# A hybrid retention and sparse-attention layer: five edits to the order of the mixer's side work

## The chip, the cores and the metric

The kernel runs on one core of a Trainium2 chip. The metric is the device time of one execution in microseconds (us); of the kernel before, the median of three runs is 1142.47 us (1141.43 to 1143.33). The engines are TensorE (PE, with weight loads as PEld), VectorE (DVE), ScalarE (ACT), GpSimd (POOL) and SyncE (SP), which issues most of the transfers. Each runs its instructions in program order and waits on semaphores for the others. Matrix products land in PSUM, eight banks of 512 fp32 columns for each partition.

## The reference, cut to what matters

One encoder layer for a prompt (512 tokens) and a sample (32 tokens), with shared weights: a feed-forward half step, a mixer, a second feed-forward half step, each followed by a LayerNorm of the residual stream. A vector c, multiplied by the matrix w_cond, gives shift, scale and gate of each step (nine pieces of 1024 columns). The mixer projects its input once and feeds two groups of heads:

```python
h = modulate(x, sh2, sc2)
z = jnp.einsum('btd,de->bte', h, w_in)      # retention q,k,v,gate | attention q,k,v | indexer q,k,weights
# retention, 4 heads: scores = (q k^T) * D ; S_new = gamma^C * S + k^T (decay * v) ; inner + q S * decay
# attention, 8 heads: rotary on 16 of 64 dims; an indexer score picks the 128 best keys of each query
s = jnp.einsum('bqhd,bsd->bqhs', iq, ik) * (IDX_DH ** -0.5)
index_score = jnp.einsum('bqh,bqhs->bqs', iw, jax.nn.relu(s))
_, idx = lax.top_k(index_score, topk)       # then softmax attention over the chosen keys
x = post_norm(x, jnp.einsum('btm,md->btd', mixed, w_out), 1.0 + gt2, 1.0, ln2_g, ln2_b)
```

The sample attends to 512 cached keys and its own 32. All is fp32.

## The kernel before, in words

Activations lie transposed, features on partitions and all 544 tokens (512 + 32) along the free dimension, in two halves of 272 columns. A weight block of 128 x 1024 is loaded in fp32 (`wr`), and split into a rounded part and a rest (`wh`): a cast on ScalarE (L131) and a subtraction on VectorE, GpSimd or in a transfer (L141, L139). Each product takes three matmuls, so a half of a block is a stretch of 8 x 3 = 24 matmuls; `in` is such a stretch of the mixer's projection. All matmuls go through `mm` (L77), transpositions through `turned` (L80), and both keep the order in which they are written. `load` keeps the order of SyncE's loads.

The work beside the projections is written as generators. `project` (L893) computes one 128-column block of the projection in two stretches and calls `tick()` after each, and every generator says with `yield n` after how many ticks it is resumed. So the number of yields sets behind which stretch a generator's matmuls stand in PE's order, and flags (`wait_for`) hold a generator until another has got to a point. Instructions of the other engines are ordered by a scheduler, from their dependencies and priorities; `behind` adds an order where one is wanted.

Around the change:

- **LayerNorm to the mixer's input** (`ln_half`, `ln_to_h`, L300-367). VectorE adds up S and Q over the features (L264, L265), PE sums them over partitions (`pm`, `pv`), a chain of small VectorE steps (L332-L341) makes the reciprocal root, then each of the eight feature blocks h_0 to h_7 gets L364 (VectorE), L366 (ScalarE) and L367 (VectorE). It is done for token half 0, then half 1; the projection of half 0 starts on h_0 and h_1 while half 1's sums run.
- **cond_ahead(7)** (L595) computes piece 7 of c times w_cond ahead of time, as eight multiply-adds over rows of w_cond, each with two VectorE instructions on 128 x 1024 (L605 for the first, L607 for the others). Below, "pieces" 0 to 7 are these eight. 0 to 3 stand ahead of the indexer's rotary turn (`rope_turn`, L926), where VectorE waits for the gathered rows; 4 to 7 stand at 502, 526, 548 and 574 us.
- **The top-k** (`topk`, L1099): 16 rounds (17 for the sample, work['s']) of MAX8 and MATCH_REPLACE8 for each query block; it yields after every second round, and after every round for 's'. The masks are then used by attention.
- **retention(hh)**, one after another for four heads. Its side generator multiplies the sample's k and q into `pz` (`rz` in the profile), VectorE multiplies that with the decay (L1200), PE transposes the sample's k into the same bank (L1201), ScalarE scales the transposition (L1202).
- **pair_inputs(c)**, four pairs of heads: projections, rotary turn, then stacks `aks`, `aqs`; it sets the flag ("stack", c), from which `attention` may start pair c. **attention** takes a pair in three steps n = 0, 1, 2 (logits of 128 and 256 columns, of 384, of 512) and a pipeline of logits (`lg`, bank tag l, two banks), transposition (`pt`, tag t, two) and values (`po`, tag o, one). VectorE reads the logits with the mask in L1278.
- **sample_attention(g)**, for pairs 2g and 2g+1: logits `sl` of the sample, softmax `Psu`, transposition `spt`, values `spo` (tag l).

Of the kernel before, what the change touches and what calls it, by code (L numbers as in the profile page):

```python
# [16 lines left out]
P = 128  # L17
# [22 lines left out]
def encoder_layer_kernel(ctx, tc, xT, cT, wc1, w_e, w_cond, b_condT, lnp, w_gu1, w_dn1, w_in, w_out, w_gu2, w_dn2,  # L40
# [525 lines left out]
    def cond(parts, gaps):  # L566
# [13 lines left out]
        for n, (m, d) in enumerate(todo):  # L580
# [11 lines left out]
                spawn(cond_done(m, accs[m]))  # L592
            yield gaps[n % len(gaps)]

    def cond_ahead(m):  # L595
        acc = [up.tile([P, 1024], F32, name=f"ca{m}_{r}", tag="u") for r in range(2)]

        def part(d):
            return w_cond[d * P:(d + 1) * P, 1024 * m:1024 * m + 1024]

        def add(d, w):
            for r in range(2):
                c = cz[:, d, r:r + 1]
                if d == 0:
                    n = nc.vector.tensor_scalar(acc[r], w, c, None, op0=ALU.mult)  # L605
                else:
                    n = nc.vector.scalar_tensor_tensor(acc[r], w, c, acc[r], op0=ALU.mult, op1=ALU.add)  # L607
                tc.add_manual_dep(n.ins, last["pe"], NOSYNC, reason="pace")

        ws = [up.tile([P, 1024], F32, name=f"wc{m}_{d}", tag="u") for d in range(4)]  # L610
        for d in range(4):
            nc.gpsimd.dma_start(ws[d], part(d))
        yield 6
        for d in range(4):
            add(d, ws[d])
            if d % 2:
                yield 1
        yield 16
        for d in range(4, ND):
            ws.append(up.tile([P, 1024], F32, name=f"wc{m}_{d}", tag="u"))  # L620
            load(ws[d], part(d))
        for d in range(4, ND):
            add(d, ws[d])
            yield 5 if d < ND - 1 else 20
        spawn(cond_done(m, acc))

    def later(n, job):
# [295 lines left out]

    def rope_turn(rp, *zs):
        r = rp[0:32 * len(zs)]
        behind(behind(nc.vector.stream_shuffle(r[:, 1, :], r[:, 0, :], SWAP), "evac"), "norm")  # L926
        nc.vector.tensor_mul(r, r, tabA[0:32 * len(zs)])
        nc.vector.tensor_add(r[:, 0, :], r[:, 0, :], r[:, 1, :])
        for slot, z in enumerate(zs):
            nc.sync.dma_start(z[ROT], rp[32 * slot:32 * slot + 32, 0, :])  # L930
# [35 lines left out]


    hls = [next_w(0) for c in range(4)]
    ensure(1)
    misc = unit("misc")  # L970
    cs = misc[:, 0, 0:12]
    load(cs, csm)
# [5 lines left out]
    tabA, tabR = unit("tabA"), unit("tabR")  # L978
    load(tabA, ropes[0])
    load(tabR, ropes[1])  # L980
    ix, ix2 = unit("ix"), unit("ix2")
    ikd = ix[:, 0, :]
    z = ikd
# [119 lines left out]
    def topk():  # L1103
        for t, rate in ((1, 2), (2, 2), (3, 2), ('s', 1)):
            while ("score", t) not in flags:
                yield 1
            w = work[t]
            for n in range(17 if t == 's' else 16):
                m8 = sm.tile([P, 8], F32, name="m8", tag="m8")
                behind(behind(nc.vector.max(m8, w), "pe"), "norm")  # L1110
                nc.vector.match_replace(w, in_to_replace=m8, in_values=w, imm_value=MARK)  # L1111
                if n % rate == rate - 1:
                    yield 1
            nc.vector.tensor_scalar(w, w, -3.3e38, NEG, op0=ALU.is_gt, op1=ALU.mult)
            if t != 's':
                L = P * (t + 1)
                nc.vector.memset(w[0:64, L - 64:L], NEG)
            flags.add(("mask", t))
# [41 lines left out]
    def retention(hh):  # L1160
        qk = unit("rqk")
        q, k = qk[:, 0, :], qk[:, 1, :]
        project_full(q)
        Dm = unit("Dm")
        Dh = Dm[:, 0, 0:P]
        load(Dh, dec[hh])
        S0 = Dm[:, 1, 0:128]
        load(S0, s0[hh])
        so, so2 = Dm[:, 1, 128:256], Dm[:, 1, 256:384]
        ss = Dm[:, 0, P:P + 32]  # L1170
        project_full(k)
        sa, sb = unit("rsA"), unit("rsB")
        sT, kt = sa[:, 0, 0:512], sa[:, 1, 0:512]
        on = sb[:, 1, 0:512]
        on2 = sb[:, 0, 256:384]
        ks = sb[:, 0, 384:512]
        vu = unit("rv")
        V = vu[:, 0, 0:512]
        vsm = vu[0:32, 1, 0:P]
        St = vu[:, 1, P:4 * P]  # L1180
        rt = ret[hh // 2][:, hh % 2, :]

        def tk(x, t):
            return x[:, t * P:(t + 1) * P]

        def side():
            yield 1 if hh else 2
            ps = bank("l", "rs")
            for t in range(4):
                mm(tk(ps, t), tk(k, t), tk(q, t), start=True, stop=True)  # L1190
            nc.vector.tensor_tensor(sT.rearrange("p (t n) -> p t n", t=4), ps.rearrange("p (t n) -> p t n", t=4),
                                    Dh.unsqueeze(1).to_broadcast([P, 4, P]), op=ALU.mult)
            pk = bank("t", "rkt")
            for t in range(4):
                turned(tk(pk, t), tk(k, t), ident)
            nc.scalar.activation(kt, pk, AF.Copy, scale=gk[:, hh:hh + 1])
            yield 1
            pz = bank("l", "rz")
            mm(pz[0:32, 0:32], k[:, TP:T], q[:, TP:T], start=True, stop=True)
            nc.vector.tensor_mul(ss[0:32], pz[0:32, 0:32], Dh[0:32, 0:32])  # L1200
            turned(pz[0:32, P:2 * P], k[:, TP:T], ident)  # L1201
            nc.scalar.activation(ks[0:32], pz[0:32, P:2 * P], AF.Copy, scale=gks[0:32, hh:hh + 1])  # L1202
            yield from wait_for(("V", hh))
            pu = bank("l", "ru")
            for t in range(4):
                mm(tk(pu, t), tk(kt, t), tk(V, t), start=True, stop=True)
            nc.vector.tensor_copy(tk(St, 0), tk(pu, 0))
            for t in range(1, 4):
                nc.vector.scalar_tensor_tensor(tk(St, t) if t < 3 else so, tk(St, t - 1), GAM[hh] ** P, tk(pu, t),
                                               op0=ALU.mult, op1=ALU.add)  # L1210
            nc.sync.dma_start(st_p[hh], so)
            yield 1
            po = bank("a", "ro")
            for t in range(4):
                mm(tk(po, t), tk(sT, t), tk(V, t), start=True, stop=(t == 0))
                if t:
                    mm(tk(po, t), tk(q, t), tk(St, t - 1), start=False, stop=True)
            po2 = bank("l", "ro2")
            mm(po2[0:32, 0:P], ss[0:32], vsm, start=True, stop=False)
            mm(po2[0:32, 0:P], q[:, TP:T], S0, start=False, stop=True)  # L1220
            ps2 = po2[:, P:2 * P]
            mm(ps2, ks[0:32], vsm, start=True, stop=True)
            nc.scalar.activation(on, po, AF.Copy, scale=gn[:, hh:hh + 1])
            nc.scalar.activation(on2[0:32], po2[0:32, 0:P], AF.Copy, scale=gn[0:32, hh:hh + 1])
            nc.vector.scalar_tensor_tensor(so2, S0, GAM[hh] ** 32, ps2, op0=ALU.mult, op1=ALU.add)
            nc.sync.dma_start(st_s[hh], so2)
            normed = [(on[:, n * P:(n + 1) * P], P) for n in range(4)] + [(on2[0:32], 32)]
            with tc.high_priority():
                w = head_norm(normed)
            yield 2  # L1230
            for j, (x, rows) in enumerate(normed):
                nc.scalar.activation(x, x, AF.Identity, bias=w[:rows, 2, j:j + 1], scale=w[:rows, 1, j:j + 1])
            yield 1
            pt = bank("t", "rot")
            for nt in range(4):
                turned(pt[:, nt * P:(nt + 1) * P], on[:, nt * P:(nt + 1) * P], ident)
            nc.scalar.activation(rt[:, 0:TP], pt, AF.Copy, scale=0.5)
            pt2 = bank("a", "rot2")
            turned(pt2[:, 0:32], on2[0:32], ident[0:32, 0:32])
            nc.scalar.activation(rt[:, TP:T], pt2[:, 0:32], AF.Copy, scale=0.5)  # L1240
            flags.add(("ret", hh))

        spawn(side())
        value_chunk(V, vsm, None, ("V", hh))

# [37 lines left out]
    def pair_inputs(c):  # L1283
# [10 lines left out]
        def roped():  # L1294
# [6 lines left out]
            parts(st[0], q)  # L1301
            for s in range(2):
                nc.gpsimd.tensor_copy(qz[own(s), 32 * s:32 * s + 32], q[own(s), TP:T])
            yield 3 if c == 0 else 1
            flags.add(("stack", c))

        Vs[c] = V
# [13 lines left out]
    def sample_attention(g):  # L1321
# [4 lines left out]
        load(cvt, cv[g])  # L1326
        if g == 0:
            yield 3
        yield from wait_for(("mask", 's'), ("att", 2 * g + 1))
        ps, p2 = bank("a", "sl"), bank("t", "sl2")  # L1330
        for j in range(4):
            c = 2 * g + j // 2
# [21 lines left out]
            nc.scalar.copy(PT2[0:32], pt2[0:32, 0:P])  # L1354
            nc.scalar.copy(PT, pt)
        yield 1
        po = bank("l", "spo")
        pcs = [po[own(j % 2), 32 * (j // 2):32 * (j // 2) + 32] for j in range(4)]
        for e in range(2):
            for t in range(4):  # L1360
# [10 lines left out]
    def attention():  # L1371
# [46 lines left out]
        while tiles or any(pipe):  # L1418
# [6 lines left out]
                values(*pipe[2])  # L1425
            if item:
                logits(*item)
            if pipe[1]:
                turn(*pipe[1])
            pipe = [item] + pipe[:2]  # L1430
# [241 lines left out]
```

## Time and profile before

| | us |
|---|---|
| median of three runs | 1142.47 |
| profiled execution | 1138.22 |
| its span, first to last instruction | 1136.4 |
| PE busy in the span | 1110.4 |
| VectorE busy | 850.0 |
| ScalarE busy | 637.1 |
| GpSimd busy | 196.7 |
| PE's waits for VectorE at `lg` / at `rz` | 5.1 / 4.1 |

The times of all rows are from one profiled execution; us count from its first instruction. "Busy" is the sum of the times in which an engine executed something. A row of a timeline gives start, length, engine, line, operation, tiles, shape and count, and in brackets how long the engine had been idle before and what it waited for. The mixer's projections run from about 404 to 690 us. The mean granted clock of TensorE is 0.993 of full speed.

### The profile page before, as it was taken

How to read it: one execution, taken by the hardware profiler on the slowest of the kernel's cores; microseconds unless marked ns; L12 is line 12 of the kernel's file. 1: busy time of each engine (PE TensorE's matmuls, PEld its weight loads, DVE VectorE, ACT ScalarE, POOL GpSimd, SP SyncE). 2: the span in 40 equal slices, each digit the busy share in tenths (PEclk: the TensorE clock that was granted, in tenths of full speed). 3: DMA queues.
4: the chain of work that ended last, by engine and by line, in shares of the span. 5: the costliest groups of instructions: out<-in, count | busy, mean ns of one | idle time of the engine just before them, and what ended most of it. 6: DMA issues, size and time to landing. Idle time of an engine off the chain costs nothing.

```text
span 1136.4 us, 22804 instructions
## 1 busy us (share of the span) xinstructions
PE 1110.4 (98%) x9059; PEld 1079.3 (95%) x9059; DVE 850.0 (75%) x1766; ACT 637.1 (56%) x1116; POOL 196.7 (17%) x217
## 2 busy tenths in 40 slices
PE   8999999999999999999989999999999999999995
PEld 7999999999999999889878989999999999999995
DVE  5578898788779796788898786799799876910416
ACT  3645656754334464766455768646666666753523
POOL 0111111121100313423110101100111111151110
PEclk9999999999999999999989999999999999999998
DMA  9798878997977455756954687861888677478842
GB/s 358 269 274 218 223 193 227 256 262 249 322 211 170 113 202 146 170 168 151 251 115 125 140 262 192 216 200 29 219 235 225 161 180 186 136 215 180 174 83 80
DMA packets 71164, 221.18 MB, mean 195 GB/s; under 512 B 8624, under 2 KB 12848, under 8 KB 71056
## 3 DMA queue, kind: packets, MB, share of 16 engines
q1 hardware_dynamic: 49456, 151.02, 38.0%
q0 software_dynamic: 21456, 68.56, 33.5%
q8 instruction: 71, 1.16, 0.4%
q14 instruction: 37, 0.30, 0.1%
q10 hardware_dynamic: 144, 0.14, 0.0%
HBM read 208.09 MB, written 9.58 MB: 192 GB/s over the span
## 4 chain that ended last, share of the span: by engine, by line
PE 87%; DVE 6%; DMA 4%; ACT 1%; issue 1%; SPq 0%; DVEq 0%; ACTq 0%
PE dn L77 27%; PE pA L77 16%; PE in L77 14%; PE gu L77 11%; PE pB L77 8%; PE pC L77 4%; DMA we_raw<-in_w_e 3%; PE gu_e L77 2%; DVE wk L1111 1%; DVE m L1110 1%; PE po L77 1%; PE lg L77 1%; PE isc L77 1%; PE pt L80 1%; PE ro L77 0%
## 5 line engine op out<-in xcount | busy, mean ns | idle before, releaser
L77 PE MATMUL dn<-hid,wh_w 128*128 128x272 f32 x2112 | 266.6, 288 | 0.0
L77 PEld LDWEIGHTS dn<-hid,wh_w 128*128 128x128 f32 x2112 | 265.2, 188 | 0.2
L77 PE MATMUL in<-h,wh_w 128*128 128x272 f32 x1392 | 188.3, 292 | 0.0
L77 PEld LDWEIGHTS in<-h,wh_w 128*128 128x128 f32 x1392 | 178.0, 190 | 5.2 <-issue 2.8
L131 ACT CAST wh_w<-wr_w 128x1024 fp32r<-128x1024 f32 (+1 forms) x102 | 102.9, 1013 | 100.1 <-PE dn L77 84.2
L77 PE MATMUL gu<-h,wh_w 128*128 128x272 f32 x960 | 121.1, 288 | 0.0
L77 PEld LDWEIGHTS gu<-h,wh_w 128*128 128x128 f32 x960 | 120.6, 188 | 0.0
L589 DVE SCALAR_TENSOR_TENSOR ca<-wc,cz,ca 128x1024 f32<-128x1024 f32 x84 | 107.4, 1298 | 0.0
L77 PE MATMUL pA<-hs,wh_s 128*128 128x272 f32 x720 | 100.3, 288 | 0.0
L77 PEld LDWEIGHTS pA<-hs,wh_s 128*128 128x128 f32 x720 | 93.8, 188 | 0.0
L138 ACT ACTIVATE wh_w<-wh_w 128x1024 fp32r<-128x1024 f32 (+1 forms) x80 | 81.5, 1023 | 1.6
L286 DVE SCALAR_TENSOR_TENSOR xs<-dn,C,xs 128x272 f32<-128x272 f32 (+2 forms) x24 | 9.0, 404 | 81.6 <-PE dn L77 81.6
L680 POOL DMA_DIRECT2D wh_g<-in_w_gu x30 | 26.1, 871 | 240.8 <-ACT wh_g L679 164.1
L714 ACT COPY s<-pA 128x272 f32<-128x272 f32 x90 | 34.5, 383 | 53.9 <-PE pA L77 53.2
L139 POOL DMA_DIRECT2D wh_w<-in_w_dn x32 | 28.2, 881 | 175.6 <-ACT wh_w L138 134.9
L703 DVE TENSOR_TENSOR wh_s<-wr_g,wh_s 128x1024 fp32r<-128x1024 f32 x30 | 36.7, 1224 | 19.4 <-ACT wh_s L702 19.4
L77 PE MATMUL pA<-h,wh_g 128*128 128x272 f32 x360 | 50.1, 288 | 0.0
L77 PE MATMUL pB<-hs,wh_u 128*128 128x272 f32 x360 | 49.8, 287 | 0.0
L77 PE MATMUL pC<-h,wh_g 128*128 128x272 f32 x360 | 49.8, 287 | 0.0
L77 PE MATMUL pB<-hs,wh_s 128*128 128x272 f32 x360 | 49.8, 287 | 0.0
L77 PE MATMUL pA<-h,wh_s 128*128 128x272 f32 x360 | 49.7, 287 | 0.0
L702 ACT CAST wh_s<-wr_g 128x1024 fp32r<-128x1024 f32 x30 | 31.5, 1050 | 30.0 <-DVE wr_g L698 30.0
(331 smaller groups left out, 2052.9 us busy)
## 6 DMA issues: line engine op xcount, KB each, us to landing
wc<-in_w_cond SPq DMA_DIRECT2D x52, 512.0 KB, 6.6
wr_w<-in_w_in SPq DMA_DIRECT2D x33, 512.0 KB, 4.6
wr_g<-in_w_gu SPq DMA_DIRECT2D x30, 512.0 KB, 3.6
wr_u<-in_w_gu SPq DMA_DIRECT2D x30, 512.0 KB, 4.4
wh_g<-in_w_gu POOLq DMA_DIRECT2D x30, 512.0 KB, 6.5
wr_w<-in_w_dn SPq DMA_DIRECT2D x32, 448.0 KB, 4.4
wh_w<-in_w_in POOLq DMA_DIRECT2D x27, 512.0 KB, 7.2
wr_w<-in_w_gu SPq DMA_DIRECT2D x24, 512.0 KB, 7.4
```

Source lines behind the costliest of these rows:

```text
L77: ordered("pe", nc.tensor.matmul(*a, **kw))
L80: ordered("pe", nc.tensor.transpose(*a))
L131: c = nc.scalar.copy(hi[:, :n, :], raw[:, :n, :])
L138: nc.scalar.mul(lo[:, :n, :], hi[:, :n, :].bitcast(F32), -1.0)
L139: nc.gpsimd.dma_start(lo[:, :n, :], src, accum_op=ALU.add)
L589: got = nc.vector.scalar_tensor_tensor(acc, ws[n], c, acc, op0=ALU.mult, op1=ALU.add)
L680: nc.gpsimd.dma_start(lo, src, accum_op=ALU.add)
L702: pin(nc.scalar.copy(W[f][:, 0], raw[f]))
L703: pin(nc.vector.tensor_tensor(W[f][:, 1], raw[f], W[f][:, 0].bitcast(F32), op=ALU.subtract))
L714: pin(nc.scalar.copy(s, ps))
L1110: behind(behind(nc.vector.max(m8, w), "pe"), "norm")
L1111: nc.vector.match_replace(w, in_to_replace=m8, in_values=w, imm_value=MARK)
```

## The change

It leaves the number of matmuls and what is computed as they are. Five edits:

1. `ensure(2)` instead of `ensure(1)`: a second w_in block is loaded and split ahead of the mixer's constants.
2. `cond_ahead`: pieces 4 and 5 follow pieces 0 to 3 at once, their two loads stand behind the rotary tables' loads on SyncE's queue (`ahead_more`), and the indexer's rotary turn is ordered behind piece 5. Pieces 6 and 7 come some 40 ticks later.
3. `topk` yields less often for the sample: 12 times in 17 rounds.
4. retention: the transposition of the sample's key is issued ahead of VectorE's reading of `pz`.
5. `pair_inputs` yields 4 instead of 3 for pair 0; `sample_attention` also waits for the flag ("lg", 2), set when the last logits of pair 2 are issued, and its values use the bank tag o instead of l.

```diff
 def cond_ahead(m):
...
+                if d < 6:
+                    last["piece"] = n.ins.name
...
-        yield 6
+
+        def more():
+            d = len(ws)
+            ws.append(up.tile([P, 1024], F32, name=f"wc{m}_{d}", tag="u"))
+            load(ws[d], part(d))
+
+        ahead_more.extend([more] * 2)
+        yield 5
         for d in range(4):
             add(d, ws[d])
             if d % 2:
                 yield 1
-        yield 16
-        for d in range(4, ND):
-            ws.append(up.tile([P, 1024], F32, name=f"wc{m}_{d}", tag="u"))
-            load(ws[d], part(d))
-        for d in range(4, ND):
+        for d in (4, 5):
             add(d, ws[d])
-            yield 5 if d < ND - 1 else 20
+        yield 40
+        more()
+        more()
+        for d in (6, 7):
+            yield 6 if d == 6 else 3
+            add(d, ws[d])
+        yield 3
         spawn(cond_done(m, acc))
...
-        behind(behind(nc.vector.stream_shuffle(r[:, 1, :], r[:, 0, :], SWAP), "evac"), "norm")
+        behind(behind(behind(nc.vector.stream_shuffle(r[:, 1, :], r[:, 0, :], SWAP), "evac"), "norm"), "piece")
...
-    ensure(1)
+    ensure(2)
...
     load(tabR, ropes[1])
+    for more in ahead_more:
+        more()
...
-                if n % rate == rate - 1:
+                if n % rate == rate - 1 if t != 's' else n % 4:
                     yield 1
...
             mm(pz[0:32, 0:32], k[:, TP:T], q[:, TP:T], start=True, stop=True)
+            turned(pz[0:32, P:2 * P], k[:, TP:T], ident)
             nc.vector.tensor_mul(ss[0:32], pz[0:32, 0:32], Dh[0:32, 0:32])
-            turned(pz[0:32, P:2 * P], k[:, TP:T], ident)
...
-            yield 3 if c == 0 else 1
+            yield 4 if c == 0 else 1
...
-        yield from wait_for(("mask", 's'), ("att", 2 * g + 1))
+        yield from wait_for(("mask", 's'), ("att", 2 * g + 1), ("lg", 2))
...
-        po = bank("l", "spo")
+        po = bank("o", "spo")
...
             if item:
                 logits(*item)
+                if item[1] == 2:
+                    flags.add(("lg", item[0]))
```

What that moves is shown at three places. The first is VectorE in the LayerNorm that makes the mixer's input, half 0: a part of its chain, between S and Q of the seventh feature block and the first `ht`. Before:

```order
L264 TENSOR_TENSOR S<-S,xa_3230 128x272
L337 TENSOR_TENSOR lnz<-pv,lny 128x272
L265 TENSOR_TENSOR Q<-Q,sq 128x272
L338 SCALAR_TENSOR_TENSOR pv<-lnz 128x272
L339 SCALAR_TENSOR_TENSOR pv<-pv,lnz 128x272
L341 SCALAR_TENSOR_TENSOR lny<-pv,lny 128x272
```

and now:

```order
L264 TENSOR_TENSOR S<-S,xa_3230 128x272
L337 TENSOR_TENSOR lnz<-pv,lny 128x272
L265 TENSOR_TENSOR Q<-Q,sq 128x272
L338 SCALAR_TENSOR_TENSOR pv<-lnz 128x272
L141 TENSOR_TENSOR wh_w<-wr_w,wh_w 128x1024
L339 SCALAR_TENSOR_TENSOR pv<-pv,lnz 128x272
L341 SCALAR_TENSOR_TENSOR lny<-pv,lny 128x272
```

A weight split (L141) has come in behind L338. Some fifteen rows further, on the same engine, come S and Q of the eighth feature block (h_5 to h_7 are feature blocks of the mixer's input). Before:

```order
L367 SCALAR_TENSOR_TENSOR h_5_4816<-ht,B_3755,h_5_4816 128x272
L364 SCALAR_TENSOR_TENSOR ht<-xa_3230,G_3754,lny 128x272 x2
L264 TENSOR_TENSOR S<-S,xa_3230 128x272
L265 TENSOR_TENSOR Q<-Q,sq 128x272
L367 SCALAR_TENSOR_TENSOR h_6_4817<-ht,B_3755,h_6_4817 128x272
L367 SCALAR_TENSOR_TENSOR h_7_4818<-ht,B_3755,h_7_4818 128x272
```

and now:

```order
L364 SCALAR_TENSOR_TENSOR ht<-xa_3230,G_3754,lny 128x272 x2
L367 SCALAR_TENSOR_TENSOR h_5_4816<-ht,B_3755,h_5_4816 128x272
L367 SCALAR_TENSOR_TENSOR h_6_4817<-ht,B_3755,h_6_4817 128x272
L367 SCALAR_TENSOR_TENSOR h_7_4818<-ht,B_3755,h_7_4818 128x272
L264 TENSOR_TENSOR S<-S,xa_3230 128x272
L265 TENSOR_TENSOR Q<-Q,sq 128x272
```

S and Q stand behind h_6 and h_7 instead of ahead of them.

The second place is VectorE at the first reads of attention's logits (pair 0; `wk_5266` is the prompt's last top-k block). Before:

```order
L1111 MATCH_REPLACE wk_5266<-m_7046,wk_5266 128x512
L1110 MAX m_7104<-wk_5266 128x8
L1278 ISA Pu,mx<-lg,wk_5266 128x128
L1278 ISA mx 128x1
L1111 MATCH_REPLACE wk_5266<-m_7104,wk_5266 128x512
L1270 TENSOR_SCALAR nm<-mx 128x1
```

and now, where `wk_5279` is that block and `wk_5278` the sample's:

```order
L1126 MATCH_REPLACE wk_5279<-m_7140,wk_5279 128x512
L1126 MATCH_REPLACE wk_5278<-m_7182,wk_5278 128x544
L1129 TENSOR_SCALAR wk_5279<-wk_5279 128x512
L1125 MAX m_7185<-wk_5278 128x8
L1132 MEMSET wk_5279 64x64
L1126 MATCH_REPLACE wk_5278<-m_7185,wk_5278 128x544
L1293 ISA Pu,mx<-lg,wk_5279 128x128
L1293 ISA mx 128x1
```

The reads stood amid the block's rounds; now they stand behind its last round, its mask and two of the sample's rounds. Piece 7 of the modulation, which stood some dozen rows ahead of the first read, is gone from there.

The third is PE around the sample's values (`spo`, g = 0). Before, they stood between the values and transpositions of pair 3:

```order
L77 MATMUL spo<-Psu,cvt 64x32 x8
L77 MATMUL spo<-PsT_8604,aV 64x32 x2
L77 MATMUL spo<-Psu,cvt 64x32 x8
L77 MATMUL spo<-PsT_8604,aV 64x32 x2
L77 MATMUL po<-Pu,aV 64x128 x6
L80 MATMUL pt<-cm,Pu 128x128 x8
```

and now ahead of pair 3's first logits:

```order
L80 MATMUL vt<-cm,vz 128x128 x4
L80 MATMUL vts<-cm,vz 32x128
L77 MATMUL spo<-Psu,cvt 64x32 x8
L77 MATMUL spo<-PsT_8322,aV 64x32 x2
L77 MATMUL spo<-Psu,cvt 64x32 x8
L77 MATMUL spo<-PsT_8322,aV 64x32 x2
L77 MATMUL lg<-aks,aqs 128x128 x6
```

The sample's part for pairs 0 and 1 is done one pair earlier than before.

More of the change, by code (lines that the diff above doesn't have):

```diff
@@ L593, in cond @@
             yield gaps[n % len(gaps)]
+    ahead_more = []
     def cond_ahead(m):
```

## The prediction

> **What bounds the kernel now.** I read the engine totals first, then TensorE's waits, then its timeline around each of them, and last VectorE's timeline ahead of them. The engine totals of the page:
>
> ```profile
> PE 1110.4 (98%) x9059; PEld 1079.3 (95%) x9059; DVE 850.0 (75%) x1766; ACT 637.1 (56%) x1116; POOL 196.7 (17%) x217
> ```
>
> TensorE (PE) is busy for 1110.4 of the span's 1136.4 us. The change leaves every matmul in place, so only the 26.0 us in which PE stands idle, and what a lowered clock costs, can move. The waits of PE, grouped by the operation that waits and the one that ends the wait (total, times, longest):
>
> ```profile
> PE lg L77 <- DVE mx L1278: 5.1, 3, 2.5
> PE rz L80 <- DVE Dm L1200: 4.1, 4, 2.8
> PE vts L80 <- ACT Pu L1398: 0.4, 1, 0.4
> ```
>
> These are the three in the mixer: attention's logits (`lg`) waiting until VectorE has read a PSUM bank, the key transposition of retention (`rz`) waiting for VectorE's reading of the score, and one small wait. Together 9.6 us; the rest of the idle time lies at the start and the end, where the change does nothing. PE's timeline shows each (start, length, instruction, then in brackets the idle time before it):
>
> ```profile
> 465.72 0.28 PE L80 MATMUL rz<-cm,rqk 128*32 128x128 f32 x1 [0.70 <-DVE Dm L1200]
> 491.92 0.28 PE L80 MATMUL rz<-cm,rqk 128*32 128x128 f32 x1 [0.34 <-DVE Dm L1200]
> 523.37 0.28 PE L80 MATMUL rz<-cm,rqk 128*32 128x128 f32 x1 [0.27 <-DVE Dm L1200]
> 550.82 0.28 PE L80 MATMUL rz<-cm,rqk 128*32 128x128 f32 x1 [2.79 <-DVE Dm L1200]
> ...
> 581.54 3.25 PE L77 MATMUL in<-h,wh_w 128*128 128x272 f32 x24
> 587.27 0.68 PE L77 MATMUL lg<-aks,aqs 64*128 64x384 f32 x1 [2.47 <-DVE mx L1278]
> 589.12 1.32 PE L77 MATMUL lg<-aks,aqs 64*128 64x384 f32 x5 [1.17 <-DVE mx L1278]
> 590.37 4.88 PE L77 MATMUL in<-h,wh_w 128*128 128x272 f32 x24
> ...
> 642.41 0.79 PE L77 MATMUL lg<-aks,aqs 64*128 64x384 f32 x6
> ...
> 675.78 1.50 PE L77 MATMUL lg<-aks,aqs 64*128 64x512 f32 x6 [1.42 <-DVE mx L1278]
> ```
>
> The pair of waits at 587 costs more than its 2.47 + 1.17 = 3.64 us: the 24 matmuls behind it take 4.88 us instead of the 3.25 of those ahead of it (+1.6), and the five `lg` 1.32 where six take 0.79 undisturbed (+0.5). That is 2.1 us of lowered clock. The windows of 5 us around both long waits (the figure behind POOL's is the granted clock):
>
> ```profile
> 545.00:550.00 5.00, 3.03 (x25) 2.71 (x24) 4.86 (x11) 2.01 (x5) 0.86 (x1) 1.00 1.05 291
> 550.00:555.00 5.00, 4.18 (x35) 4.17 (x35) 4.86 (x13) 1.22 (x3) 0.00 (x0) 1.00 1.05 309
> 585.00:590.00 5.00, 1.56 (x6) 1.10 (x6) 5.00 (x22) 3.48 (x8) 0.87 (x1) 0.72 0.35 72
> 590.00:595.00 5.00, 5.00 (x27) 4.63 (x24) 4.64 (x17) 0.49 (x2) 0.00 (x0) 0.60 0.61 105
> ```
>
> The idle 2.79 us before 550.82 left the clock at 1.00, while the 3.64 us broken by one matmul took it to 0.72 and 0.60.
>
> **The retention swap.** PE's order is the same; what changes is that the transposition no longer follows VectorE's reading of the score in the same bank, but goes ahead of it. All four waits go: 0.70 + 0.34 + 0.27 + 2.79 = 4.1 us. In exchange VectorE's reading (now L1216) waits for one 0.28 us transposition, which ends long before VectorE arrives (head 3: VectorE came 2.79 us after PE). ScalarE's scaled copy of the key (now L1217) has to wait for VectorE instead; behind it on ScalarE are the copies of the value chunk, for matmuls that follow 3.24 us of other work, and it starts no later than before, since before it waited for the same VectorE instruction and a transposition besides. Price: -4.1 us, nothing next in line.
>
> **One more w_in block before the gap.** With `ensure(2)` a block's split, one ScalarE cast and one VectorE subtraction (L141), stands in the middle of the LayerNorm that makes the mixer's input, half 0. VectorE's rows there:
>
> ```profile
> 398.71 0.44 DVE L338 SCALAR_TENSOR_TENSOR pv<-lnz 128x272 f32<-128x272 f32 x1
> ...
> 406.54 0.43 DVE L264 TENSOR_TENSOR S<-S,xa 128x272 f32<-128x272 f32 x1
> 407.24 0.91 DVE L367 SCALAR_TENSOR_TENSOR h<-ht,B,h 128x272 fp32r<-128x272 f32 x2
> ...
> 421.93 1.22 DVE L141 TENSOR_TENSOR wh_w<-wr_w,wh_w 128x1024 fp32r<-128x1024 f32 x1
> ```
>
> and PE's, at the sum over the features (`pm`) that reads S:
>
> ```profile
> 407.03 0.72 PE L77 MATMUL pm<-S,cm 128*128 128x272 f32 x2
> ```
>
> Before, S was ready at 406.54 + 0.43 = 406.97 and PE read it at 407.03: no reserve. Now an L141 (1.22) stands behind L338, and the two L367 that stood behind S (0.91) stand ahead of it. S comes 1.22 + 0.91 = 2.13 later, less about 0.3 for starts that overlap the end of the one before: PE waits 1.85 us that it didn't wait before. Ends: 0.8 us if only the L367 are felt, since the L141 falls into a pause; 2.2 if nothing overlaps. I take 1.85, near the upper end, since VectorE's rows are back to back. The block's load is no part of it: it stands ahead of the mixer's constants on SyncE's queue. The other half's LayerNorm starts later by as much, loses the L141 at 421.93, and PE reaches it later by as much: nothing.
>
> **Two pieces of modulation in the gap.** VectorE stands idle before the rotary shuffle, and six instructions of the same kind give the price of one:
>
> ```profile
> 424.93 7.25 DVE L607 SCALAR_TENSOR_TENSOR ca<-wc,cz,ca 128x1024 f32<-128x1024 f32 x6
> 439.19 0.01 DVE L926 LOAD_MASK_SELECT rp<-rp  x1 [6.43 <-DMA rp<-iqf]
> ```
>
> Four more take 4 x 7.25 / 6 = 4.83 us, in 6.43 us of idle time that the L141 moved away widens: free, as long as the gathered rows don't arrive over 1.6 us earlier; if they do, the rest falls on the indexer's rope, with no PE wait near it in the list above. Their two loads stand on SyncE's queue behind the rotary tables, and one w_in load fewer stands just ahead of the gathers. The pieces leave their old places, and that is what pays at head 3 and in the first attention. Pieces 6 and 7 go into attention's pairs 2 and 3, where VectorE still has pauses; the second of these rows shows one, 1.85 us:
>
> ```profile
> 573.55 1.27 DVE L607 SCALAR_TENSOR_TENSOR ca<-wc,cz,ca 128x1024 f32<-128x1024 f32 x1
> 639.32 0.29 DVE L1278 CUSTOM_DVE_ANT_0 Pu<-lg,wk 128x128 f32<-128x128 f32 x1 [1.85 <-PE lg L77]
> ```
>
> **The first attention.** Logits now start one 24-matmul stretch later, so PE, which was through with the stretch ahead of the second group (`lg` on 384 columns) at 581.54 + 3.25 = 584.8, comes there at 584.8 + 3.2 = 588.0 in the old times. It needs both PSUM banks of the first group read. VectorE's order is new: the reads no longer stand amid the top-k rounds but behind all of them, with two rounds of the sample's top-k pulled in by the faster yield. These rows price that (the first round stands behind the rope, the last row is the last read of the first group before):
>
> ```profile
> 568.52 0.69 DVE L1110 MAX8 m<-wk 128x8 f32<-128x512 f32 x1
> ...
> 581.28 0.69 DVE L1110 MAX8 m<-wk 128x8 f32<-128x512 f32 x1
> 582.80 0.69 DVE L1110 MAX8 m<-wk 128x8 f32<-128x512 f32 x1
> ...
> 588.64 0.42 DVE L1278 CUSTOM_DVE_ANT_0 Pu<-lg,wk 128x256 f32<-128x256 f32 x1
> ```
>
> Nothing changes up to 573.55, where piece 7 stood. From there 8 rounds of the prompt and 2 of the sample at 582.80 - 581.28 = 1.52 us make 15.2, less an estimated 0.7 where another instruction fills the pause inside a round; the two rope results 1.2; the mask's end 0.45: the first read comes at 589.7. Three reads later, of 0.42 us at most, the first bank is free: 590.7. PE waits 590.7 - 588.0 = 2.7, with the second bank 3.0 us, where it waited 3.64. Ends: 2.0 if more rounds overlap, 4.2 if the rotated keys land 1.2 us late. Without a drop of the clock the 2.1 us go too.
>
> The clock is the open part. [...] So I let it keep the clock, by the row nearest in length, at little better than even odds.
>
> **Pairs 1 to 3 and the sample.** The wait of 1.42 us at 675.78 goes: the sample's two reads stood between the two `lg` reads of pair 3 and now stand in pair 2. The 0.41 us on ScalarE in pair 1 becomes about 0.5, between 0 and 1.7 (the 1.85 us pause is the reserve that a later start uses up). In pair 2 the sample's output bank is now shared with attention's own, so PE waits until VectorE has read that; I count about 1.8 us of reserve there (rival 3).
>
> **Sum**, against the profiled execution of 1138.22 us (span 1136.4, 1.8 around it): -4.1 (retention) - 0.64 - 2.1 (first attention and its clock) - 1.42 (pair 3) + 0.1 (pair 1) + 1.85 (LayerNorm) = -6.3 us, so 1131.9. The median of the runs is 4.25 above that execution, 1142.47; the same difference gives **1136.2 us**. A measurement of this kernel can tell 0.2%, 2.3 us, from nothing.
>
> **Rivals.** *1, the clock still falls in the first attention (0.30).* For it: 3.64 us in all did it before, and 3.0 is near. Then the 2.1 us stay: -4.2, 1138.3. [...]
>
> *2, the first attention doesn't wait (0.10).* If the rounds overlap as the interleaved ones do and the keys land early, VectorE is 3 us sooner: -9.3, 1133.2. Against it: ten rounds in a row depend each on the one before.
>
> *3, slower: the shared output bank (0.06).* In pair 2 the sample's values wait for VectorE's reading of attention's output, which stands behind piece 7, the sample's softmax and the rope of pair 3, and that one waits for a DMA. VectorE is in order, so a late DMA holds it all, and then the logits behind PE's wait. The row before:
>
> ```profile
> 653.65 0.70 DVE L928 TENSOR_TENSOR rp<-rp 64x544 f32<-64x544 f32 x1
> 658.44 0.67 DVE L949 TENSOR_TENSOR aks<-aqk,aks 128x512 fp32r<-128x512 f32 x1
> ```
>
> gave 658.44 - 654.35 = 4.1 us and no wait. Every us beyond my reserve of 1.8 is PE's, and a wait past 3.6 brings 2.1 of clock. To come out over 2.3 us slower it must eat 6.3 + 2.3 - 2.1 = 6.5 us: the DMA 8.3 us later than now, 12.4 in all. At that, 1144.8.
>
> *4, it moves waits and gains little (0.10).* The new wait in the LayerNorm at 2.2, the first attention at 4.2 with its clock drop, pair 1 at 1.7: -4.1 + 0.6 - 1.42 + 1.3 + 2.2 = -1.4, 1141.1.
>
> **How the numbers follow.** My case has 0.44, the rivals 0.30, 0.10, 0.06 and 0.10. The range runs from rival 2, 1133.2, less 0.7 for the LayerNorm's low end, to just under rival 4: 1132.5 to 1141.0. Faster by over 2.3 us (below 1140.2) are my case and rivals 1 and 2, less 0.03 for their tails: 0.81; rival 4 and these tails are within 0.2%: 0.13; rival 3 is slower: 0.06.
>
> **What would show it.** In the new profile PE's list has no `rz` row; a row `pm` waiting for S of about 1.9 us stands near 407; `lg` waits for VectorE once, about 3 us near 585, with 24 matmuls behind it at 3.25 us (4.88 if rival 1 holds); no `lg` wait in pair 3; no `spo` row. The forecast is wrong if `pm` doesn't wait, if `spo` or `spt` does, or if PE's idle time in the mixer is over 8 us.

## The result, and the profile after

The changed kernel takes 1135.05 us (median of four runs, 1134.79 to 1135.26) where the kernel before took 1142.9 (four runs, 1141.43 to 1143.62). The ratio is 0.9933 with a 95% interval of 0.9916 to 0.995: 7.85 us less, between 5.7 and 9.6. Forecast were 1136.2 and -6.3 us. That the numbers lie near each other is partly chance: two terms of the forecast were wrong, in opposite directions, as the part on the prediction shows.

The profiled execution of the changed kernel took 1134.79 us, its span is 1133.0. The engine totals:

```profile
PE 1110.3 (98%) x9059; PEld 1079.8 (95%) x9059; DVE 850.6 (75%) x1766; ACT 636.8 (56%) x1116; POOL 196.3 (17%) x217
```

No engine does less work; PE is idle 22.7 us instead of 26.0. PE's waits in the mixer, out of the same grouping as before:

```profile
PE lg L77 <- DVE mx L1293: 3.5, 2, 3.2
PE pm L77 <- DVE S L264: 1.5, 1, 1.5
...
PE pt L80 <- ACT Pu L1413: 0.6, 1, 0.6
```

The `rz` row is gone, `pm` is new, and `pt`, which waits for ScalarE's copy of a transposition in pair 2, was not foreseen. PE's timeline at these places:

```profile
408.95 0.73 PE L77 MATMUL pm<-S,cm 128*128 128x272 f32 x2 [1.52 <-DVE S L264]
...
582.16 3.26 PE L77 MATMUL in<-h,wh_w 128*128 128x272 f32 x24
588.64 1.73 PE L77 MATMUL lg<-aks,aqs 64*128 64x384 f32 x6 [3.22 <-DVE mx L1293]
590.30 5.31 PE L77 MATMUL in<-h,wh_w 128*128 128x272 f32 x24
...
639.31 1.19 PE L77 MATMUL lg<-aks,aqs 64*128 64x384 f32 x6 [0.26 <-DVE mx L1293]
651.31 0.55 PE L80 MATMUL pt<-cm,Pu 128*128 128x128 f32 x3 [0.57 <-ACT Pu L1413]
```

The wait at the second logits group is one piece of 3.22 us now, and the clock falls behind it as it did before: the 24 matmuls that follow take 5.31 us, those ahead 3.26. The windows (the granted clock is the figure behind POOL's):

```profile
585.00:590.00 5.00, 1.78 (x10) 1.30 (x8) 5.00 (x24) 2.11 (x8) 0.08 (x1) 0.81 0.60 105
590.00:595.00 5.00, 5.00 (x24) 4.70 (x22) 5.00 (x21) 0.95 (x4) 0.00 (x0) 0.51 0.00 0
```

Between the two profiled executions the time falls by 1138.22 - 1134.79 = 3.4 us. The mixer's waits make -4.0 of it: -4.1 at `rz`, -1.6 at `lg` (5.1 to 3.5), -0.4 at `vts`, +1.5 at `pm`, +0.6 at `pt`. What PE loses behind the waits of the first attention is nearly the same in both. Without the idle time, its six `lg` and the 24 matmuls behind them take 6.75 us before and 6.90 now (counted to the starts of the next rows, 595.19 and 595.54), where they take 3.9 undisturbed: a loss of 2.8 and of 3.0 us. Some 0.4 us of such a loss is put down to the wait and not to the clock, an estimate from one row: behind a wait of 0.76 us six such `lg` take 1.20 us at a clock of 1.00 (the sample's top-k one tick later, below), and 0.79 undisturbed. At the start of the program, where no edit stands, PE's waits at the modulation (`c`) came out 0.9 us longer. That makes -4.0 + 0.2 + 0.9 = -2.9; where the remaining 0.5 us are is not shown. The other 4.4 us of the 7.85 are not between these two profiles: the kernel before has a median 4.7 us above its profiled execution, the changed one 0.26 us above its own.

### The profile page after: what moved, and what is told of

It reads as the page before. It is cut to its first block, busy times and chain, and to the rows that moved or that the text cites. A ratio compares the mean times of both kernels' runs of the same rounds, so it can differ in the third digit from the quotient of the medians.

```text
span 1133.0 us, 22791 instructions
## 1 busy us (share of the span) xinstructions
PE 1110.3 (98%) x9059; PEld 1079.8 (95%) x9059; DVE 850.6 (75%) x1766; ACT 636.8 (56%) x1116; POOL 196.3 (17%) x217
## 4 chain that ended last, share of the span: by engine, by line
PE 86%; DVE 7%; DMA 5%; ACT 1%; issue 1%; SPq 0%; DVEq 0%; ACTq 0%
PE dn L77 26%; PE pA L77 16%; PE in L77 13%; PE gu L77 11%; PE pB L77 8%; PE pC L77 4%; DMA we_raw<-in_w_e 3%; PE gu_e L77 2%; DVE m L1125 1%; DVE wk L1126 1%; DMA aqk<-rp 1%; PE isc L77 1%; PE ro L77 1%; PE lg L77 1%; PE pt L80 1%
```

## The experiments

Each was timed against the kernel before on the same chip; the ratios are to that. The changed kernel wasn't timed again beside them. The kernel before has medians of 1140.2 to 1141.4 us in these sessions, against 1142.9 in the four runs of the result, so one or two us between one of these runs and the changed kernel are not told apart.

**The kernel before, again, twice.** No edit.

> The kernel before, unchanged, a second time. Its first profiled execution took 1138.2 us while its timed runs took 1141.4 to 1143.6. Theory A (the granted clock falls at a second place in most executions, the 2.8 us wait of retention head 3, and didn't in that one): a profiled execution at 1141 to 1143 us shows a window with a clock of about 0.5 to 0.8 behind 550 us and a slow stretch of 24 matmuls (about 4.9 instead of 3.25 us) there. Theory B (the profiled execution differs in something spread over the whole span, such as transfers at the start): no new place with a lowered clock, and the 4 us stand elsewhere. If this execution is at 1138 again, the two stay open.

> The kernel before once more, for a profile of one of its longer executions (both profiled ones took 1138.2 us, the median is near 1141). If the granted clock falls behind the 2.8 us wait of retention head 3 in those: a window near 550 us at about 0.6, the 24 matmuls there at 4.5 to 5 us, and the mixer longer by 2 to 3 us. Rival: the extra time stands behind the waits of attention (587 or 676 us) or ahead of the mixer. If the profiled execution is a short one again, only the list of times and clocks can speak: time should go up by 2.5 to 3.5 us for each 0.002 that the mean clock falls.

The first: 1140.09 us (ten runs, 1138.18 to 1144.03), ratio 0.9992 (0.9974 to 1.0009), profiled at 1138.18, so as before. The second: 1140.47 (1137.28 to 1144.78), ratio 0.9999 (0.998 to 1.0017), profiled at 1139.18 with a mean clock of 0.991. This profile bears on theory A. PE's timeline there:

```profile
550.59 0.28 PE L80 MATMUL rz<-cm,rqk 128*32 128x128 f32 x1 [2.80 <-DVE Dm L1200]
550.63 4.79 PE L77 MATMUL in<-h,wh_w 128*128 128x272 f32 x24
```

and the window, here and in the first repetition:

```profile
550.00:555.00 5.00, 4.41 (x23) 4.41 (x24) 4.86 (x13) 0.36 (x1) 0.00 (x0) 0.66 1.04 309
```

```profile
550.00:555.00 5.00, 4.12 (x34) 4.11 (x35) 4.86 (x13) 1.17 (x3) 0.00 (x0) 1.00 1.04 305
```

The same kernel, the same wait of 2.8 us, and once the clock stays at 1.00, once it falls to 0.66 and 24 matmuls take 4.79 instead of 3.24 us. So theory A holds for this place: retention's last wait costs 2.8 us in some executions and 4.35 in others. It isn't all of the spread. Of the 85 timed executions of the kernel before on these three chips, the 23 with a mean clock of 0.993 or more have a median of 1139.5 us, the 47 with 0.991 or 0.992 one of 1140.5, the 15 below that one of 1143.6. No profile shows one of the last. The median of all 85 is 1140.5, and only 30 of them reach 1141.43, the lowest of the result's four. Against 1140.5 the changed kernel's 1135.05 would be 5.5 us less, not 7.85.

**The retention swap alone, and everything but the swap.** In the first, the kernel before with only this; in the second, the changed kernel with the opposite:

```diff
+            turned(pz[0:32, P:2 * P], k[:, TP:T], ident)
             nc.vector.tensor_mul(ss[0:32], pz[0:32, 0:32], Dh[0:32, 0:32])
-            turned(pz[0:32, P:2 * P], k[:, TP:T], ident)
```

> The kernel before with the retention swap alone. Theory A (the four waits go, and in the timed runs a drop of the clock at head 3 with them): 4.1 us and 2 to 4 of clock, so about 1135 to 1137 us where before takes 1142.5, and a profiled execution without an rz wait. Theory B (only the 4.1 us of waits): 1138 to 1139. Rival (VectorE passes the delay on to the first attention, which waits longer): 1140 to 1142.

> The changed kernel with the retention swap undone. If the swap carries most of the gain: the four rz waits are back, 4.1 us or more, so 1139 us or more. Rival (the wait of head 3 came from modulation piece 6 standing on VectorE just ahead of the score's reading, and that piece is gone from there): only the three small waits of together 1.3 us come back, 1136 to 1137 us, and no rz wait is over 1 us.

The swap alone: 1133.72 us (nine runs, 1133.03 to 1138.13) where before took 1141.38, ratio 0.9941 (0.9923 to 0.9958). No `rz` row; what is left waits for attention's logits:

```profile
583.71 0.44 PE L77 MATMUL lg<-aks,aqs 64*128 64x384 f32 x1 [2.90 <-DVE mx L1278]
585.56 1.20 PE L77 MATMUL lg<-aks,aqs 64*128 64x384 f32 x5 [1.41 <-DVE mx L1278]
586.69 4.37 PE L77 MATMUL in<-h,wh_w 128*128 128x272 f32 x24
```

That is theory A, which has 5.5 to 7.5 us: the four waits of 4.1 us are worth 6.7 us by the ratio. Three of the nine runs took 1137 to 1138 us, at a mean clock of 0.991 where the others have 0.993 or 0.994; what lowers it in these, no profile shows. Everything but the swap: 1137.04 us, ratio 0.9963 (0.9948 to 0.9978), which is 2.0 us more than with it by the times and 3.4 by the ratios. Its profile is of the longest of its eleven executions (1142.43 us), so only the waits at `rz` are read from it. The wait of head 3 is 0.54 us there, not 2.79:

```profile
554.66 0.28 PE L80 MATMUL rz<-cm,rqk 128*32 128x128 f32 x1 [0.54 <-DVE Dm L1215]
```

So the rival holds in this one. In the kernel before, the two instructions of modulation piece 6 stand on VectorE just ahead of the score's reading:

```profile
547.69 1.27 DVE L607 SCALAR_TENSOR_TENSOR ca<-wc,cz,ca 128x1024 f32<-128x1024 f32 x1
...
549.40 1.28 DVE L607 SCALAR_TENSOR_TENSOR ca<-wc,cz,ca 128x1024 f32<-128x1024 f32 x1
550.60 0.17 DVE L1200 TENSOR_TENSOR Dm<-rz,Dm 32x32 f32<-32x32 f32 x1
```

They make 2.55 us, and with the piece elsewhere 2.25 of the 2.79 us are gone. The swap takes away the rest and the three small waits (1.3 us). The two edits overlap, and their gains don't add.

**The changed kernel without the early block.**

```diff
-    ensure(2)
+    ensure(1)
```

> The changed kernel with ensure(1) as before. If the split in the LayerNorm costs what the profile shows at pm (1.5 us) and brings nothing: the pm wait goes and the time falls by 1.5 us to about 1133.5. Rival (the early block is needed to keep the gap before the rotary turn free for pieces 4 and 5): the split comes back ahead of the pieces, the shuffle comes later, and the time stays or rises by up to 2 us.

1138.73 us, ratio 0.9973 (0.9959 to 0.9986): slower than the changed kernel by 3.7 us by the times, and by more than the rival had. The `pm` wait is gone, but PE now waits for the block's split, which VectorE does behind all the pieces in the gap. VectorE's rows, then PE's:

```profile
424.44 12.04 DVE L609 SCALAR_TENSOR_TENSOR ca<-wc,cz,ca 128x1024 f32<-128x1024 f32 x10
...
439.50 1.21 DVE L141 TENSOR_TENSOR wh_w<-wr_w,wh_w 128x1024 fp32r<-128x1024 f32 x1
```

```profile
440.77 5.52 PE L77 MATMUL in<-h,wh_w 128*128 128x272 f32 x31 [4.04 <-DVE wh_w L141]
```

The clock falls behind this wait (0.66 from 440 to 445 us): 31 matmuls of this shape take 4.13 us elsewhere in this profile and 5.52 here. The early block is what makes the gap usable: 1.5 us at `pm` are the price for not paying 4.0 and the fall here.

**The early block, split without VectorE.** In the changed kernel:

```diff
-        queue_w(w_in[c], lo_eng=nc.vector if c in (4, 17) else None)
+        queue_w(w_in[c], lo_eng=nc.vector if c == 4 else None)
```

> The changed kernel, with the lower half of the second w_in block made by ScalarE and an accumulating transfer instead of VectorE's subtraction (L141). If that subtraction in the LayerNorm's chain is what delays S: the wait of 1.5 us at pm falls to under 0.5, and the time by 1 to 1.5 us, to about 1133.8. Rival (the order of S and Q behind h_6 and h_7 does it, and it stays): still about 0.8 us of wait, 1134.5. If the transfer comes late, a wait at the first matmul that uses the block, up to 4 us.

1133.56 us (four runs, 1131.76 to 1135.14), ratio 0.9935 (0.9911 to 0.9959). The wait at the second `pm` is gone, and the time is about what the first theory has, though the interval doesn't part it from the changed kernel. The profile has a wait of 1.49 us at the first `pm` instead, 16 us earlier and ahead of this edit's work. Two other profiles of this study have a wait there too (2.07 without the swap, 1.41 with attention's start as before), and the one with both edits, below, has none at either `pm`. So VectorE's subtraction makes the second wait, and not the order of S and Q, which was the rival. What makes the first, and whether it varies with the execution, isn't shown:

```profile
392.38 0.72 PE L77 MATMUL pm<-S,cm 128*128 128x272 f32 x2 [1.49 <-DVE S L264]
...
408.59 0.73 PE L77 MATMUL pm<-S,cm 128*128 128x272 f32 x2
```

**The sample's top-k one tick later**, alone and with the edit above:

```diff
+            if t == 's':
+                yield 1
             w = work[t]
```

> The changed kernel, with the sample's top-k starting one tick later, so that none of its rounds stands ahead of the first reads of attention's logits. If the 3.2 us wait at the second logits group comes from these two rounds (3.0 us) and the mask's end (0.4): that wait is under 0.5 us, no window there has a lowered clock (the 24 matmuls behind it at 3.25 instead of 5.31 us), together 5 to 6 us: about 1129.5. Rival (VectorE is behind by more than these rounds, or the sample's mask, a tick later, makes PE wait in pair 2): a gain of under 2 us, 1133 to 1136.

> The two edits of the runs above together. If they act on separate waits, their gains add: 1128 to 1129 us, and PE's waits in the mixer are under 1.5 us in all. [...]

Alone: 1137.36 us, ratio 0.9962 (0.9945 to 0.9978). The wait of 3.22 us fell to 0.76 (the first theory had under 0.5) with a clock of 1.00, and two waits of together 1.08 us came up at the logits of 512 columns. Yet the time rose, beyond what either had. The rows show where it went:

```profile
586.38 1.20 PE L77 MATMUL lg<-aks,aqs 64*128 64x384 f32 x6 [0.76 <-DVE mx L1295]
...
638.33 1.73 PE L77 MATMUL lg<-aks,aqs 64*128 64x384 f32 x6 [2.48 <-DVE mx L1295]
639.99 5.37 PE L77 MATMUL in<-h,wh_w 128*128 128x272 f32 x24
```

Pair 2 now waits, 2.48 us, and the clock falls there (0.53 from 640 to 645 us). So the rounds were what held the reads of pair 0, and VectorE's work was only put off. With both edits: 1133.18 us, ratio 0.993 (0.9911 to 0.9949), no better than the block's split alone (1133.56), so the gains don't add. The wait in pair 2 is 1.29 us. What VectorE did ahead of it, from the same profile:

```profile
627.27 0.69 DVE L962 TENSOR_TENSOR aks<-aqk,aks 128x512 fp32r<-128x512 f32 x1 [3.00 <-ACT aks L961]
...
631.68 2.47 DVE L609 SCALAR_TENSOR_TENSOR ca<-wc,cz,ca 128x1024 f32<-128x1024 f32 x2
...
634.71 0.27 DVE L1295 CUSTOM_DVE_ANT_0 Pu<-lg,wk 128x128 f32<-128x128 f32 x1
```

It stood idle for 3.00 us, and then did piece 6 for 2.47 us just ahead of the reads.

**Piece 6 into that idle time.** To both edits above:

```diff
-        yield 40
+        yield 38
```

> The kernel with the sample's rounds a tick later and the block split by a transfer, and pieces 6 and 7 two ticks earlier (38, not 40). There VectorE stood idle for 3.0 us waiting for the rotated keys of pair 2, and then did piece 6 (2.5 us) just ahead of pair 2's first reads, where PE waited 1.3 us. If piece 6 fits into that gap: that wait goes, with the lowered clock behind it, 2 to 3 us: 1130 to 1131. Rival (piece 7, earlier too, now stands between pair 2's reads): a wait of as much at its 384 or 512 columns, and no gain, 1133.

1132.64 us (four runs, 1131.96 to 1133.72), ratio 0.9928 (0.9907 to 0.995), profiled at 1131.96 with a span of 1130.1. The lowest median of the study, though not told apart from the kernel with both edits (1133.18), nor from the changed kernel, whose ratio is 0.9933. PE's longest wait for VectorE in the mixer is 0.9 us, and the clock stays at 1.00 from 350 to 740 us:

```profile
PE lg L77 <- DVE mx L1295: 2.7, 4, 0.9
...
PE vt L80 <- ACT Pu L1415: 1.1, 1, 1.1
```

The first theory's 1130 to 1131 us were not reached, and the rival was right in part: 0.87 us stand at pair 2's 512 columns now. A wait of 1.1 us for ScalarE (`vt`) is new.

**Attention's start as before**, in the changed kernel:

```diff
-            yield 4 if c == 0 else 1
+            yield 3 if c == 0 else 1
```

> The changed kernel with attention's start for pair 0 as before (3 ticks, not 4). If PE's later arrival is what shortens the wait at the second logits group: PE comes 3.2 us earlier, and waits up to 6.4 us instead of 3.2, so 1138 us or more. Rival (VectorE's order goes with it: the reads then stand two rounds further ahead, amid the block's rounds, as before): 3 to 4 us of wait and about the same time, 1134.5 to 1136.

1136.33 us, ratio 0.9962 (0.9947 to 0.9976). The wait is 3.10 us, not 6.4: the rival. The time is just above the rival's 1136; this profile also waits 1.41 and 1.73 us at the two `pm`. VectorE's order goes along with PE's, and starting attention later buys nothing at this wait.

**The swap with the block and the pieces, and the sample's part as before.** The first is the kernel before with edits 1, 2 and 4 alone; the second the changed kernel with

```diff
-        yield from wait_for(("mask", 's'), ("att", 2 * g + 1), ("lg", 2))
+        yield from wait_for(("mask", 's'), ("att", 2 * g + 1))
...
-        po = bank("o", "spo")
+        po = bank("l", "spo")
```

> The kernel before with the retention swap, ensure(2) and the moved pieces, without the edits to the top-k's rate, attention's start and the sample. Theory (the swap carries the gain; the pieces' move saves nothing by itself, since the first attention's reads still stand amid the rounds and PE comes early, and it costs the 1.5 us at pm): 1 to 2 us slower than the swap alone, about 1135 to 1136, with some 3.5 us of wait at the second logits group. Rival (piece 7 gone from VectorE shortens that wait by its 2.5 us and frees the clock): 1130 to 1132.

> The changed kernel with the sample's edits undone (its logits amid pair 3, its output in a bank of the logits). If moving it is what removed the wait at the logits of 512 columns in pair 3: a wait of 1.2 to 1.7 us is back there, 1136.5 us. Rival (that wait went because VectorE is less behind): no wait over 0.5 us there, and the same time, 1135.

The first: 1136.4 us, ratio 0.9972 (0.9957 to 0.9987), above the swap alone (0.9941), as the theory had it, though not for all of its reasons. Moving piece 7 away does shorten the first attention's waits, to 3.10 + 0.16 us where the swap alone has 2.90 + 1.41. That 1.0 us is lost again at `pm` (1.52) and in pair 3, where the wait is as long as ever and the clock falls behind it (0.73 from 670 to 675 us).

```profile
585.50 0.44 PE L77 MATMUL lg<-aks,aqs 64*128 64x384 f32 x1 [3.10 <-DVE mx L1293]
...
671.98 2.18 PE L77 MATMUL lg<-aks,aqs 64*128 64x512 f32 x6 [1.82 <-DVE mx L1293]
```

The second: 1136.57 us, ratio 0.9955 (0.994 to 0.9971). The time is the first theory's, the wait isn't: in pair 3 only 0.49 us show, nearer the rival:

```profile
674.39 0.95 PE L77 MATMUL lg<-aks,aqs 64*128 64x512 f32 x5 [0.49 <-DVE mx L1293]
```

The profiles without the early block and with the sample's rounds a tick later have the same 0.49 us there, with the sample's edits in place. So most of the 1.42 us is gone with the sample's reads in their old place. What is left as a cause is the faster rate, attention's start or both, which may have freed VectorE at that point. The profile with attention's start as before has 0.28 us there, which points to the rate; the rate alone wasn't tried.

## Why the prediction was right, and where it wasn't

**Retention, -4.1 us: right in the waits, too small in time.** All four waits went. The term lacked the clock: the forecast read from one profile that 2.79 us of idle time leave it at 1.00, and the second repetition shows that they don't always (0.66). The swap alone is worth 6.7 us, and it is the whole result as far as the intervals tell: 0.9941 alone, 0.9933 with the four other edits, one inside the other's interval.

**From the execution to the median: wrong.** "The same difference gives 1136.2" took the 4.25 us between the profiled execution and the median as a property of the measurement. It was a property of the kernel before, whose clock falls in some executions and not in others (0.66 and 1.00 behind the wait of head 3), and of the three runs it was taken from: over the 85 later executions the difference is 2.3. The changed kernel's four runs lie within 0.5 us. This step made the forecast 4.0 us too high.

**The first attention: rival 1.** The wait was priced at 3.0 us and is 3.22. That the clock would be kept, as behind the 2.79 us of head 3 and at little better than even odds, was wrong: 0.81 and 0.51. The term was also too small as it stood. Its 2.1 us set five `lg` at 1.32 us against six at 0.79 and left out the sixth, which alone took 0.68; counted whole, 2.8 us are lost before and 3.0 now. So the forecast took off 2.1 where 0.2 came on, 2.3 us too low. By profiled executions alone the forecast was -6.3 and rival 1 -4.2; measured is -3.4. The forecast was thus 2.9 us too low for the profiled execution and 4.0 too high in the step to the median, which leaves the 1.1 by which 1136.2 missed: luck.

**The LayerNorm, +1.85: right, 1.52.** The forecast's reading of S behind L141 and two more L367 holds row for row. What it missed is what this buys. It priced the block as a loss and the pieces as free; without the block PE waits 4.04 us for the split behind the pieces. The gap was also fuller than thought: of 6.43 us of idle time 0.34 are left, by VectorE's rows of the changed kernel.

```profile
426.82 12.04 DVE L609 SCALAR_TENSOR_TENSOR ca<-wc,cz,ca 128x1024 f32<-128x1024 f32 x10
439.20 0.01 DVE L939 LOAD_MASK_SELECT rp<-rp  x1 [0.34 <-DMA rp<-iqf]
```

**The pieces leaving their places as "what pays at head 3 and in the first attention": half right.** At head 3 it does (0.54 us left without the swap), but the swap had that already. In the first attention it shortens the waits by 1.0 us (3.26 where the swap alone has 4.31) and doesn't keep the clock (0.69 from 585 to 590 us with the swap, the block and the pieces).

**Pair 3, -1.42: right in size, wrong in cause.** The sample's reads were not most of it. **Pair 1** and **the shared bank** (rival 3): pair 1's 0.4 us went instead of growing to 0.5, and there is no `spo` row. The `pt` wait of 0.57 us on ScalarE in pair 2 was in no part of the forecast. In the range, "0.7 for the LayerNorm's low end" should have been 1.85 - 0.8 = 1.05, which would move the lower bound to 1132.2.

## What to carry to other kernels

A wait of the bounding engine was not worth its length alone here: the same 2.8 us cost 2.8 in one execution and 4.35 in another. So price the clock behind a wait too, from the profile's rows, and look at more than one execution before taking it as kept or lost. When two edits relieve the same wait, time each without the other; here one line gave the whole gain as far as the timing can tell, and where the other edits were tried they mostly moved VectorE's backlog from one place to the next. An edit that looks like a loss beside the one it came with may be its cover; undoing it alone shows that.

## What the runs showed of the hardware

The length of a wait alone didn't decide here whether the clock fell. Two waits of 2.79 and 2.80 us in the same place kept 1.00 and lost it to 0.66. 1.52 us at `pm` in the changed kernel kept 1.00 (405 to 415 us), while 1.29 us in pair 2 of the kernel with both edits brought 0.70 in the window:

```profile
635.00:640.00 5.00, 4.34 (x21) 3.87 (x22) 5.00 (x28) 2.44 (x10) 0.00 (x0) 0.70 0.53 96
```

Behind 1.82 us in pair 3 (the swap with the block and the pieces) it was 0.73, behind 2.48 us in pair 2 (the sample's top-k one tick later) 0.53. In the 24 matmuls behind the waits of pair 0 a fall cost 1.1 us (the swap alone, 4.37 for 3.25) to 2.1 us (the changed kernel, 5.31 for 3.26). What decides, no run shows.
